# Folding a per-feature norm weight and bias into the product that follows it, and padding the main buffers to multiples of 512 bytes

## The chip, the cores and the metric

The kernel runs on one core of a Trainium2 chip. The metric is device microseconds of one execution; lower is better. Five engines share the work: TensorE (PE), VectorE (DVE), ScalarE (ACT), GpSimd (POOL) and SyncE (SP), which issues most of the DMAs; POOL issues the others. SBUF is the on-chip memory of 128 partitions, and PSUM holds what PE accumulates.

## The reference

One inference step of a two-layer backbone on 128 prompt tokens and 512 latent tokens of width 1024. A layer projects the modulated input, lets four mixers (windowed attention, a gated MLP over chunks, retention, pooling) work on a quarter of the columns each, joins them in an output projection and a layer norm, and ends with a gated convolutional feed-forward network. The change sits in mixer B, the gated MLP:

```
def spatial_gating(u, v, nw, nb, ws, bs):          # u, v: tokens x 256; ws: 4 x 128 x 128; bs: 4 x 128
    v = layer_norm(v, nw, nb)                      # (v - mean) * rstd * nw + nb, over 256 features
    for each chunk of 128 tokens and each head h of 64 features:
        s[i, :] = sum_j ws[h, i, j] * v[j, head h] + bs[h, i]
    return u * s
```

All of it is in fp32.

## The kernel before

The 640 tokens are five tiles of 128 columns (tile 0 is the prompt, tiles 1 to 4 are latent). Activations lie with features on partitions: `y8`, `hh` and `hl` are 128 x 8 x 640. A matmul in fp32 accuracy is made of three with rounded operands: the activation is held as a high part `hh` and a rest `hl`, a weight as `wh` and `wl` (`split`, L275 on ACT and L276 on DVE, from the staging tile `st`), and each product is hh·wh, hh·wl and hl·wh. Lines L601 to L603 (tile `fm`) do so for feature-major outputs, in two pieces of 384 columns (GA) and 256 columns (GB); L883 to L885 (`tm`) for token-major ones; L1497 to L1499 (`wo`) for the output projection; L1588 to L1590 (`dn`) for the feed-forward's second matrix.

The order on each engine is the order in which `mixers` and its helpers are written out; each engine works through its own instructions in that order. Helpers that don't depend on one another run as generators, one piece at every `tick()`.

In mixer B, `sgu_setup` loads the mixing weights, their bias `bs`, and `nwb`: nw and nb copied to all 128 partitions (L742, L743). It transposes the weights on PE (L749) and copies them to SBUF as `wsTs` (ACT, L751). Later `vb_out` takes each token tile's v out of PSUM, `vb_norm` normalizes it in three operations, 128 tokens on partitions by 256 features:

```
V.tensor_scalar(out=v, in0=v, scalar1=mv[:, 0:1], scalar2=r, op0=ALU.subtract, op1=ALU.mult)   # L908, DVE
G.tensor_tensor(out=v, in0=v, in1=m.nwb[:, 0, :], op=ALU.mult)                                 # L909, POOL
G.tensor_tensor(out=v, in0=v, in1=m.nwb[:, 1, :], op=ALU.add)                                  # L910, POOL
```

The factor `r` is one over the standard deviation, a power on POOL (`rstd_of`, L443, tile `rs`). A tile's normalization is written one tile late (`m.owed`), so that on POOL the three kinds stand mixed with the retention gates of `ret_gates` (L1071, L1072), which multiply and add 128 x 128 tiles. `sgu` (L939, tile `sg`) is the mixing on PE, 20 matmuls (40 in the trace's count) for the five tiles; DVE adds `bs` (L942) and `sgu_gate` multiplies with u (L947). The second half of u's product (GB, L601 to L603), one piece of the next layer's modulation matrix (L263, tile `ada`) and the output projection follow on PE.

Of the kernel before, what the change touches and what calls it, by code (L numbers as in the profile page):

```python
# [8 lines left out]
F32 = mybir.dt.float32  # L9
F32R = mybir.dt.float32r  # L10
AF = mybir.ActivationFunctionType
ALU = mybir.AluOpType
AX = mybir.AxisListType

P = 128
# [6 lines left out]
HD = 64  # L22
# [8 lines left out]
NT = 5  # L31
SPLIT_COL = 384
UW = 664

C_ID, C_BD, C_MASK, C_RELF, C_TRIF, C_RELB, C_TRIB = 0, 128, 256, 896, 1024, 1152, 1280
C_IQ, C_KC, C_COS, C_SIN, C_PF = 1408, 1664, 1666, 2178, 2690
# [3 lines left out]
def tcol(t):  # L40
    return t * P
# [48 lines left out]
def kernel(  # L90
# [6 lines left out]
    V, S, G, T = nc.vector, nc.scalar, nc.gpsimd, nc.tensor  # L97
    load, side = nc.sync.dma_start, nc.gpsimd.dma_start

    NW, NU = 12, 25  # L100
    one = ctx.enter_context(tc.tile_pool(name="one", bufs=1))
    par = ctx.enter_context(tc.tile_pool(name="par", bufs=2))
# [9 lines left out]
    def nm(p):  # L112
        cnt[0] += 1
        return f"{p}{cnt[0]}"

    def unit(shape, name="u"):
        u = up.tile([P, UW], F32, tag="u", name=nm(name))[:, 0:math.prod(shape[1:])]
        if len(shape) == 3:
            u = u.rearrange("p (a b) -> p a b", b=shape[2])
        elif len(shape) == 4:  # L120
            u = u.rearrange("p (a b c) -> p a b c", b=shape[2], c=shape[3])
        return u
# [4 lines left out]
    def bank(n=512, name="m"):  # L127
        return pp.tile([P, 512], F32, tag="m", name=nm(name))[:, 0:n]


    ident = one.tile([P, P], F32, name="ident")
    bd = one.tile([P, P], F32, name="bd")
    epsb = one.tile([P, 1], F32, name="epsb")
    mhalf = one.tile([P, 4], F32, name="mhalf")
    hh = one.tile([P, KD, W], F32R, name="hh")
    hl = one.tile([P, KD, W], F32R, name="hl")
    y8 = one.tile([P, KD, W], F32, name="y8")
# [6 lines left out]
    folds = [one.tile([P, 4], F32, name="fold4"), one.tile([P, 2], F32, name="fold2")]  # L144
    sb0 = one.tile([P, 2, KD, 2], F32, name="sb0")
    bf = one.tile([P, 2, KD], F32, name="bf")
    hhf = hh.bitcast(F32)

    V.memset(scT, 0.0)
    V.memset(epsb, EPS)  # L150
    V.memset(mhalf, -0.5)


    class Cols:
        n = 2
# [4 lines left out]
        def dma(self):  # L160
            self.st = stg.tile([P, KD, 256], F32, tag="st", name=nm("st"))
            load(out=self.st, in_=self.src[:, self.c0:self.c0 + 256].rearrange("(k p) c -> p k c", p=P))
# [28 lines left out]
    class AdaFirst:  # L191
# [17 lines left out]
        ps = None  # L209
# [31 lines left out]
    class AdaPair:  # L241

        n = 1
# [155 lines left out]
    def params(l, dma):  # L399
        rows = unit([P, P], name="prow")  # L400
        dma(out=rows[0:16, :], in_=ln_w[l].rearrange("a (m p) -> (a m) p", p=P))
        dma(out=rows[16:32, :], in_=ln_b[l].rearrange("a (m p) -> (a m) p", p=P))
        dma(out=rows[32:34, :], in_=pool_scale[l].rearrange("(m p) -> m p", p=P))
        dma(out=rows[34:38, :], in_=ret_gn_w[l].rearrange("a (m p) -> (a m) p", p=P))
        cr = unit([P, 2, P], name="crow")
        dma(out=cr[0:88, 0, :], in_=ffn_conv_w[l, 0:2].rearrange("t (f p) -> (t f) p", p=P))
        dma(out=cr[0:44, 1, :], in_=ffn_conv_w[l, 2].rearrange("(f p) -> f p", p=P))
        dma(out=cr[44:88, 1, :], in_=ffn_conv_b[l].rearrange("(f p) -> f p", p=P))
        return rows, cr

    def params_tiles():
        return (par.tile([P, 38], F32, tag="prm", name=nm("prm")),
                par.tile([P, 4, 44], F32, tag="cwT", name=nm("cwT")))

    def params2(rc, prm, cwT):
        rows, cr = rc
        pt = bank(name="prT")
        T.transpose(pt[:, 0:38], rows[0:38, :], ident[0:38, 0:38])
        T.transpose(pt[:, 128:216], cr[0:88, 0, :], ident[0:88, 0:88])
        T.transpose(pt[:, 256:344], cr[0:88, 1, :], ident[0:88, 0:88])  # L420
        V.tensor_copy(out=prm, in_=pt[:, 0:38])
        V.tensor_copy(out=cwT[:, 0:2, :], in_=pt[:, 128:216].rearrange("p (t f) -> p t f", t=2))
        V.tensor_copy(out=cwT[:, 2:4, :], in_=pt[:, 256:344].rearrange("p (t f) -> p t f", t=2))

# [181 lines left out]
    def fm_mm(u, lo, hi):  # L606
        return fm_mms([u], lo, hi)[0]
# [124 lines left out]
                         scale=iq[:, 256 + d:257 + d])  # L732
        V.tensor_scalar(out=m.kd, in0=m.kd, scalar1=0.125, scalar2=None, op0=ALU.mult)

    def sgu_setup(m, l):
        w = unit([P, 4, P], name="ws")
        side(out=w, in_=sgu_ws[l].rearrange("h i j -> i h j"))
        m.bs = unit([P, 2, P], name="bs")
        for h in range(4):
            side(out=m.bs[(h % 2) * HD:(h % 2) * HD + HD, h // 2, :], in_=sgu_bs[l, h].partition_broadcast(HD))  # L740
        m.nwb = unit([P, 2, 256], name="nwb")
        side(out=m.nwb[:, 0, :], in_=sgu_nw[l].partition_broadcast(P))  # L742
        side(out=m.nwb[:, 1, :], in_=sgu_nb[l].partition_broadcast(P))  # L743
        yield
        yield
        yield
        pt = bank(name="wsT")
        for h in range(4):
            T.transpose(pt[:, h * P:(h + 1) * P], w[:, h, :], ident)  # L749
        m.wsT = unit([P, 4, P], name="wsTs")  # L750
        S.activation(out=m.wsT, in_=pt.rearrange("p (h i) -> p h i", h=4), func=AF.Copy)  # L751

    def pool_setup(m, l, dma):
        m.pw = par.tile([P, 2, HD], F32, tag="pw", name=nm("pw"))
        dma(out=m.pw, in_=pool_w[l].rearrange("(t a) c d -> (a c) t d", a=2))
        m.pf = par.tile([P, 2, 2, 8], F32, tag="pf", name=nm("pf"))
        dma(out=m.pf, in_=consts[:, C_PF:C_PF + 32].rearrange("p (t e c) -> p t e c", t=2, e=2))
# [144 lines left out]
    def vb_norm(m):  # L902

        if m.owed is None:
            return
        t, v, mv, r = m.owed
        m.owed = None
        V.tensor_scalar(out=v, in0=v, scalar1=mv[:, 0:1], scalar2=r, op0=ALU.subtract, op1=ALU.mult)  # L908
        G.tensor_tensor(out=v, in0=v, in1=m.nwb[:, 0, :], op=ALU.mult)  # L909
        G.tensor_tensor(out=v, in0=v, in1=m.nwb[:, 1, :], op=ALU.add)  # L910
        m.vn[t] = v

    def vc_out(m, t, ps):
# [18 lines left out]
    def sgu(m):  # L932
        for t0, n in ((0, 1), (1, 4)):
            for p in range(2):
                ps = bank(n * P, name="sg")
                for i in range(n):
                    for a in range(2):
                        h = 2 * p + a
                        T.matmul(ps[a * HD:(a + 1) * HD, i * P:(i + 1) * P], m.vn[t0 + i][:, h * HD:(h + 1) * HD],  # L939
                                 m.wsT[:, h, :], start=True, stop=True, tile_position=(0, a * HD))  # L940
                c0 = tcol(t0)
                V.tensor_tensor(out=y8[:, 2 + p, c0:c0 + n * P].rearrange("p (n i) -> p n i", n=n),  # L942
                                in0=ps.rearrange("p (n i) -> p n i", n=n),
                                in1=m.bs[:, p:p + 1, :].to_broadcast([P, n, P]), op=ALU.add)

    def sgu_gate(p, ps, lo, hi):
        V.tensor_tensor(out=y8[:, 2 + p, lo:hi], in0=ps, in1=y8[:, 2 + p, lo:hi], op=ALU.mult)  # L947
# [143 lines left out]
    def pool_in(ps_a, ps_b):  # L1091
        x = unit([P, 664], name="px")
        for a, b in ((0, 8), (136, 144), (656, 664)):
            G.memset(x[:, a:b], 0.0)
        S.activation(out=x[:, 8:136], in_=ps_a[:, 0:P], func=AF.Copy)
        S.activation(out=x[:, 144:400], in_=ps_a[:, P:SPLIT_COL], func=AF.Copy)
        S.activation(out=x[:, 400:656], in_=ps_b, func=AF.Copy)
        return x
# [44 lines left out]
    def lane(*gens):  # L1143
        lanes.append(list(gens))
# [18 lines left out]
    def mixers(l, m, prm, begun=None, aff=None):  # L1163
        dma = side if l else load
# [69 lines left out]
        ps = fm_mm(u, *GA)  # L1234
        S.activation(out=m.kc[0][:, 0:SPLIT_COL], in_=ps, func=AF.Copy)
        tick()
        ps = fm_mm(u, *GB)
# [8 lines left out]
        ps = fm_mm(u, *GA)  # L1246
# [5 lines left out]
        ps = fm_mm(u, *GB)  # L1252
# [6 lines left out]
        for i in range(2):  # L1259
            m.qc.append(keep(unit([P, W], name="qc")))  # L1260
            if i == 0 and aff:
                lane(affine_late(*aff))
        lane(sgu_setup(m, l))
        for d in range(2):
            for p in range(2):
                g = y8[:, 4 + p, :] if d == 0 else unit([P, W], name="g")
                u = ws.take()
                for lo, hi in (GA, GB):
                    ps = fm_mm(u, lo, hi)
                    S.activation(out=g[:, lo:hi], in_=ps, func=AF.Silu)  # L1270
                    if hi == W:
                        G.tensor_scalar(out=g, in0=g, scalar1=prm[:, 34 + d * 2 + p:35 + d * 2 + p], scalar2=None,
                                        op0=ALU.mult)
# [5 lines left out]
        for i in range(2):  # L1279
# [4 lines left out]
            x = pool_in(pa, pb)  # L1284
# [6 lines left out]
        uu = [ws.take(), ws.take()]  # L1291
        pa = [fm_mm(u, *GA) for u in uu]
        sgu(m)
        for p in range(2):
            sgu_gate(p, pa[p], *GA)
# [4 lines left out]
        for p in range(2):  # L1300
            ps = fm_mm(uu[p], *GB)
# [158 lines left out]
    h_first((4, 5, 6, 7), SEG_B, (G, V))  # L1460
    states()
    rc = params(0, load)
    prm, cwT = params_tiles()
    late += [lambda: params2(rc, prm, cwT)]
    load(out=bd, in_=consts[:, C_BD:C_BD + P])

    for l in range(DEPTH):
        m = Mix() if l else m0
# [15 lines left out]
        for h in range(2):  # L1484
# [5 lines left out]
            for t in range(NT):  # L1490
                c0 = tcol(t)
                if h == 0 and 0 < t < NT - 1:
                    y_split(t + 1)
                ps = bank(name="wo")
# [47 lines left out]
        for i, (br, f) in enumerate(order):  # L1542
            u = ws.take()
            ps = fm_mm(u, *GA)
# [22 lines left out]
        if nxt:  # L1567
            rc = params(l + 1, side)
            flush(True)
            sb = mods(adas[l + 1], (prm[:, 8:16], prm[:, 24:32]), 0)  # L1570
# [78 lines left out]
        if nxt:  # L1649
# [3 lines left out]
            prm, cwT = prm2, cwT2  # L1653
# [34 lines left out]
```

## Time and profile before

| what | before |
|---|---|
| median of 3 runs | 1563.03 us (1561.6 to 1563.06) |
| the profiled execution | 1563.34 us, span 1561.6 us |
| PE busy | 1529.7 us, 98% of the span |
| DVE, ACT, POOL busy | 959.5, 609.9, 379.7 us |
| mean granted TensorE clock | 0.994 of full |

The span is the time from the first to the last instruction of the profiled execution. A releaser is what an engine's idle time ended with. The granted clock of a stretch is the share of full speed at which TensorE was let run: 1.00 is 2.4 GHz and 0.50 is 1.2 GHz.

### The profile page before, as it was taken

What the parts mean: (1) busy time and instruction counts of PE and PEld (TensorE: products, weight loads), DVE (VectorE), ACT (ScalarE), POOL (GpSimd) and SP (SyncE); (2) the same over time, 40 slices, a digit from 0 to 9 for tenths busy, and PEclk for the clock granted to TensorE, in tenths of its full rate; (3) what the DMA queues carried; (4) which work ended last, traced back from release to release, by engine and by line L of the source; (5) the groups of instructions that cost most, each with busy time, mean ns of one, the idle gap of its engine ahead of it and who ended that gap; (6) DMA issues with size and microseconds to landing.
All of it is one profiled execution on the core that took longest, in us unless ns stands there. A gap on an engine that the chain in (4) does not pass through costs nothing.

```text
span 1561.6 us, 24577 instructions
## 1 busy us (share of the span) xinstructions
PE 1529.7 (98%) x9734; PEld 1358.4 (87%) x9734; DVE 959.5 (61%) x1891; ACT 609.9 (39%) x993; POOL 379.7 (24%) x458
## 2 busy tenths in 40 slices
PE   8999999999999999999999999899999999999997
PEld 5988878899999999988789988688999999998885
DVE  4775346786556655745577665567866666674456
ACT  2544462344333333533346443524433333343331
POOL 0302266054101101200013033823531101020104
PEclk9999999999999999999999999999999999999999
DMA  9644415245343443333216355161332221224311
GB/s 326 211 152 129 136 55 202 73 130 189 120 151 116 155 137 134 109 117 124 72 38 220 123 163 175 62 202 55 126 104 82 81 81 56 81 93 130 132 38 67
DMA packets 123343, 193.22 MB, mean 124 GB/s; under 512 B 11884, under 2 KB 80566, under 8 KB 123229
## 3 DMA queue, kind: packets, MB, share of 16 engines
q1 hardware_dynamic: 114701, 166.64, 32.1%
q0 software_dynamic: 8528, 25.03, 5.0%
q8 instruction: 76, 1.25, 0.3%
q14 instruction: 38, 0.31, 0.1%
HBM read 177.97 MB, written 13.66 MB: 123 GB/s over the span
## 4 chain that ended last, share of the span: by engine, by line
PE 86%; DVE 4%; POOL 4%; ACT 2%; DMA 2%; issue 1%; SPq 0%; POOLq 0%; ACTq 0%; DVEq 0%
PE fm L601 17%; PE fm L603 16%; PE fm L602 16%; PE dn L1590 6%; PE dn L1588 6%; PE dn L1589 6%; PE ada L263 2%; PE wo L1497 2%; PE wo L1498 2%; PE wo L1499 2%; POOL on L1071 1%; DVE wl L276 1%; PE po L873 1%; PE PT L858 1%; DMA st<-in_w_in_dram 1%
## 5 line engine op out<-in xcount | busy, mean ns | idle before, releaser
L601 PE MATMUL fm<-hh,wh 128*128 128x256 f32 (+1 forms) x1888 | 589.8, 312 | 0.0
L603 PE MATMUL fm<-hl,wh 128*128 128x256 f32 (+1 forms) x1888 | 583.1, 309 | 0.9 <-DVE hl L586 0.9
L602 PE MATMUL fm<-hh,wl 128*128 128x256 f32 (+1 forms) x1888 | 582.9, 309 | 0.0
L276 DVE TENSOR_TENSOR wl<-st,wh 128x1024 fp32r<-128x1024 f32 x188 | 282.7, 1512 | 164.9 <-ACT wh L275 161.8
L601 PEld LDWEIGHTS fm<-hh,wh 128*128 128x128 f32 x1888 | 356.7, 189 | 28.1 <-ACT cv L1328 11.7
L603 PEld LDWEIGHTS fm<-hl,wh 128*128 128x128 f32 x1888 | 356.6, 189 | 1.8 <-DVE hl L586 1.1
L602 PEld LDWEIGHTS fm<-hh,wl 128*128 128x128 f32 x1888 | 356.8, 189 | 0.1
L275 ACT ACTIVATE wh<-st 128x1024 fp32r<-128x1024 f32 x188 | 196.1, 1053 | 207.2 <-PE dn L1589 141.8
L1318 DVE SCALAR_TENSOR_TENSOR cv<-fm,cwT,cv 128x127 f32<-128x127 f32 x352 | 122.0, 408 | 108.3 <-ACT cv L1315 108.2
L1590 PE MATMUL dn<-wh,hl 128*128 128x512 f32 x440 | 174.0, 395 | 0.3 <-DVE hl L1524 0.2
L1588 PE MATMUL dn<-wh,hh 128*128 128x512 f32 x440 | 174.1, 396 | 0.0
L1589 PE MATMUL dn<-wl,hh 128*128 128x512 f32 x440 | 173.8, 395 | 0.0
L1315 ACT ACTIVATE cv<-fm,cwT 128x384 f32<-128x384 f32 x88 | 58.8, 673 | 203.3 <-PE fm L603 187.8
L1537 POOL TENSOR_TENSOR act<-cv,cv 128x640 f32<-128x640 f32 x28 | 45.9, 1641 | 300.3 <-DVE cv L1333 247.3
L1328 ACT ACTIVATE cv<-fm,cwT 128x255 f32<-128x255 f32 x88 | 49.6, 563 | 175.8 <-PE fm L603 175.8
L1590 PEld LDWEIGHTS dn<-wh,hl 128*128 128x128 f32 x440 | 82.5, 187 | 21.4 <-DVE hl L1524 1.2
L1589 PEld LDWEIGHTS dn<-wl,hh 128*128 128x128 f32 x440 | 82.5, 187 | 20.0
L1588 PEld LDWEIGHTS dn<-wh,hh 128*128 128x128 f32 x440 | 82.5, 187 | 19.6
L1329 DVE SCALAR_TENSOR_TENSOR cv<-fm,cwT,bnd 128x1 f32<-128x1 f32 x88 | 19.1, 217 | 89.0 <-ACT cv L1328 88.9
L1537 POOL TENSOR_TENSOR y<-cv,cv 128x640 f32<-128x640 f32 x16 | 26.8, 1678 | 182.3 <-DVE cv L1333 162.6
L1497 PE MATMUL wo<-wh,hh 128*128 128x512 f32 x160 | 64.1, 401 | 0.0
L1498 PE MATMUL wo<-wl,hh 128*128 128x512 f32 x160 | 63.2, 395 | 0.0
(306 smaller groups left out, 2036.1 us busy)
## 6 DMA issues: line engine op xcount, KB each, us to landing
st<-in_ffn_up_dram SPq DMA_DIRECT2D x44, 1024.0 KB
wa<-in_w_ada_dram SPq DMA_DIRECT2D x80, 512.0 KB
st<-in_ffn_down_dram SPq DMA_DIRECT2D x88, 256.0 KB
st<-in_w_in_dram SPq DMA_DIRECT2D x20, 1024.0 KB
xr<-xd POOLq DMA_DIRECT2D x30, 256.0 KB, 8.1
wf<-in_w_first_dram SPq DMA_DIRECT2D x24, 256.0 KB
st<-in_w_out_dram SPq DMA_DIRECT2D x24, 256.0 KB
xd<-xr SPq DMA_DIRECT2D x20, 256.0 KB
```

Of the source, the lines that this page charges most:

```text
L275: S.activation(out=oh, in_=view, func=AF.Copy)
L276: eng.tensor_tensor(out=ol, in0=view, in1=of, op=ALU.subtract)
L601: T.matmul(ps, wh[:, k, :], hh[:, k, lo:hi], start=(k == 0), stop=False)
L602: T.matmul(ps, wl[:, k, :], hh[:, k, lo:hi], start=False, stop=False)
L603: T.matmul(ps, wh[:, k, :], hl[:, k, lo:hi], start=False, stop=(k == KD - 1))
L1318: V.scalar_tensor_tensor(out=o[:, a + d:b - 1 + d], in0=ps[:, a + 1 - d:b - d], scalar=cwT[:, tap, f:f + 1], in1=o[:, a + d:b - 1 + d], op ...
L1497: T.matmul(ps, hh[:, k, c0:c0 + P], wh[:, k % 2, :], start=(k == 0), stop=False)
L1498: T.matmul(ps, hh[:, k, c0:c0 + P], wl[:, k % 2, :], start=False, stop=False)
L1537: G.tensor_tensor(out=dst, in0=a, in1=g, op=ALU.mult)
L1588: T.matmul(ps, hh[:, s_, c0:c0 + P], wh[:, k % 2, :], start=(k == 0), stop=False)
L1589: T.matmul(ps, hh[:, s_, c0:c0 + P], wl[:, k % 2, :], start=False, stop=False)
L1590: T.matmul(ps, hl[:, s_, c0:c0 + P], wh[:, k % 2, :], start=False, stop=(k == KF - 1))
```

## The change

It has two parts. In the first, v is only normalized, and nw and nb come in behind the mixing. Since nw and nb are per feature, the mixing's output is sum_j ws[i, j] * vn[j] times nw, plus nb times the row's sum of ws, plus bs. A feature is a partition there, so nw becomes a per-partition scalar, and the add of L942 becomes one operation that multiplies and adds. The rest, nb times the row sum plus bs, is made once a layer: four matmuls of `wsTs` with a tile of ones (`wsum`) and two operations on DVE. nw and nb come in as four more rows of the small parameter tile `prm`, and `nwb` goes. In the second part two tiles that nothing reads (`pad`, 320 bytes a partition, and `pad2`, 160 bytes) move the addresses of those allocated behind them: in the built program `hh`, `hl` and `y8` began 192 bytes past a multiple of 512 and now begin at one; the staging tiles and the weight tiles wh and wl began 224 bytes past one and now begin at one.

```diff
+PAD1, PAD2 = 80, 40
...
+    pad = one.tile([P, PAD1], F32, name="pad")
     hh = one.tile([P, KD, W], F32R, name="hh")
...
+    pad2 = one.tile([P, PAD2], F32, name="pad2")
+    ones = one.tile([P, HD], F32, name="ones")
+    V.memset(ones, 1.0)
+    for x in (pad, pad2):
+        V.memset(x, 0.0)
...
+        dma(out=rows[38:40, :], in_=sgu_nw[l].rearrange("(m p) -> m p", p=P))
+        dma(out=rows[40:42, :], in_=sgu_nb[l].rearrange("(m p) -> m p", p=P))
...
-    def sgu_setup(m, l):
+    def sgu_setup(m, l, prm):
...
-        m.nwb = unit([P, 2, 256], name="nwb")
-        side(out=m.nwb[:, 0, :], in_=sgu_nw[l].partition_broadcast(P))
-        side(out=m.nwb[:, 1, :], in_=sgu_nb[l].partition_broadcast(P))
...
+        yield
+
+        ps = bank(256, name="wsum")
+        for h in range(4):
+            T.matmul(ps[(h % 2) * HD:(h % 2) * HD + HD, (h // 2) * P:(h // 2) * P + P], ones, m.wsT[:, h, :],
+                     start=True, stop=True, tile_position=(0, (h % 2) * HD))
+        for p in range(2):
+            V.scalar_tensor_tensor(out=m.bs[:, p, :], in0=ps[:, p * P:(p + 1) * P], scalar=prm[:, 40 + p:41 + p],
+                                   in1=m.bs[:, p, :], op0=ALU.mult, op1=ALU.add)
+        m.nw = prm[:, 38:40]
...
-        G.tensor_tensor(out=v, in0=v, in1=m.nwb[:, 0, :], op=ALU.mult)
-        G.tensor_tensor(out=v, in0=v, in1=m.nwb[:, 1, :], op=ALU.add)
...
-                V.tensor_tensor(out=y8[:, 2 + p, c0:c0 + n * P].rearrange("p (n i) -> p n i", n=n),
-                                in0=ps.rearrange("p (n i) -> p n i", n=n),
-                                in1=m.bs[:, p:p + 1, :].to_broadcast([P, n, P]), op=ALU.add)
+                V.scalar_tensor_tensor(out=y8[:, 2 + p, c0:c0 + n * P].rearrange("p (n i) -> p n i", n=n),
+                                       in0=ps.rearrange("p (n i) -> p n i", n=n), scalar=m.nw[:, p:p + 1],
+                                       in1=m.bs[:, p:p + 1, :].to_broadcast([P, n, P]), op0=ALU.mult, op1=ALU.add)
```

On POOL the order in layer 0, at the last two normalizations, was this (`y` is a part of y8 used as scratch, `vn` the normalized v, `g` a retention gate):

```order
L443 TENSOR_TENSOR rs_2546<-rsv_2544,mhalf 128x1
L1071 TENSOR_TENSOR on_2445<-on_2445,y_86 128x128
...
L1072 TENSOR_TENSOR y_86<-on_2445 128x128
L909 TENSOR_TENSOR vn_2484<-vn_2484,nwb_1602 128x256
L910 TENSOR_TENSOR vn_2484<-vn_2484,nwb_1602 128x256
L443 TENSOR_TENSOR rs_2590<-rsv_2588,mhalf 128x1
L909 TENSOR_TENSOR vn_2579<-vn_2579,nwb_1602 128x256
L910 TENSOR_TENSOR vn_2579<-vn_2579,nwb_1602 128x256
L394 DMA gate_2768<-gs_892 128x512
```

In the changed kernel (line numbers are its own) the same place reads:

```order
L452 TENSOR_TENSOR rs_2503<-rsv_2501,mhalf 128x1
L452 TENSOR_TENSOR rs_2552<-rsv_2550,mhalf 128x1
L1085 TENSOR_TENSOR on_2455<-on_2455,y_87 128x128
...
L1086 TENSOR_TENSOR y_87<-on_2455 128x128
L452 TENSOR_TENSOR rs_2594<-rsv_2592,mhalf 128x1
L401 DMA gate_2770<-gs_900 128x512
```

The powers and the gates have kept their order; the ten operations of L909 and L910 in each layer are gone from between them.

On PE the only new rows are those of `wsum`. In layer 1 they stand behind two transposes of attention weights (`PT`), between the two pieces of a projection:

```order
L611 MATMUL fm_9200<-hh,wl_8706 128x384
L612 MATMUL fm_9200<-hl,wh_8705 128x384
L874 MATMUL PT_9226<-ident,P_9039 128x128
L874 MATMUL PT_9226<-ident,P_9045 128x128
L762 MATMUL wsum_9234<-wsTs_9188,ones 64x128 x4
L610 MATMUL fm_9241<-hh,wh_8705 128x256
L611 MATMUL fm_9241<-hh,wl_8706 128x256
```

In layer 0 they stand at the same place of the projection, without the transposes. On DVE the two operations that fold `wsum` into `bs` stand, in layer 0, behind the attention's normalization and ahead of a weight's `wl`:

```order
L865 TENSOR_SCALAR P_1777<-P_1777,su_1849 128x128
L765 SCALAR_TENSOR_TENSOR bs_1605<-wsum_1860,prm_524,bs_1605 128x128 x2
L283 TENSOR_TENSOR wl_1963<-st_1530,wh_1962 128x1024
```

There are 70 microseconds and more between that place and the first use of `bs`.

## Rows read from the trace of the kernel before

**Rows 1.** The page, part 1: TensorE.

```profile
PE 1529.7 (98%) x9734; PEld 1358.4 (87%) x9734; DVE 959.5 (61%) x1891; ACT 609.9 (39%) x993; POOL 379.7 (24%) x458
```

**Rows 2.** Waits of PE: total us, times, longest us.

```profile
PE sg L939 <- POOL vn L910: 7.2, 3, 3.9
...
PE sc L822 <- DVE qs L644: 3.2, 2, 2.4
PE PT L858 <- DVE P L849: 1.6, 1, 1.6
```

**Rows 3.** PE's timeline at both mixings: start, us, instruction, count, idle before.

```profile
241.37 1.31 PE L939 MATMUL sg<-wsTs,vn 128*64 128x128 f32 x20
244.82 1.45 PE L939 MATMUL sg<-wsTs,vn 128*64 128x128 f32 x20 [2.14 <-POOL vn L910]
...
1008.35 1.09 PE L939 MATMUL sg<-wsTs,vn 128*64 128x128 f32 x16
...
1014.99 2.40 PE L939 MATMUL sg<-wsTs,vn 128*64 128x128 f32 x20 [3.89 <-POOL vn L910]
```

**Rows 4.** Stretches: length, busy PE, PEld, DVE, ACT, POOL (counts); clock; DMA share, GB/s.

```profile
82.00:85.41 3.41, 3.41 (x16) 1.63 (x16) 2.28 (x4) 2.85 (x5) 1.46 (x3) 0.50 0.12 42
...
241.37:245.85 4.48, 2.34 (x39) 2.10 (x40) 4.48 (x5) 0.00 (x0) 4.31 (x4) 1.00 0.03 6
245.85:249.26 3.41, 3.41 (x20) 3.10 (x17) 2.52 (x6) 0.78 (x1) 3.25 (x7) 0.50 0.94 257
...
1013.85:1020.68 6.83, 5.69 (x35) 5.36 (x36) 5.20 (x9) 1.51 (x2) 5.88 (x10) 0.50 0.69 166
```

**Rows 5.** PE's timeline behind both mixings: projection GB and the modulation piece.

```profile
249.44 0.28 PE L601 MATMUL fm<-hh,wh 128*128 128x256 f32 x1
...
253.23 0.27 PE L603 MATMUL fm<-hl,wh 128*128 128x256 f32 x1
253.44 1.06 PE L263 MATMUL ada<-wa,scT 128*32 128x512 f32 x8
...
1024.68 1.06 PE L263 MATMUL ada<-wa,scT 128*32 128x512 f32 x8
```

**Rows 6.** POOL's timeline ahead of both mixings.

```profile
239.69 0.74 POOL L910 TENSOR_TENSOR vn<-vn,nwb 128x256 f32<-128x256 f32 x1
240.39 0.55 POOL L443 TENSOR_TENSOR rs<-rsv,mhalf 128x1 f32<-128x1 f32 x1
241.46 1.64 POOL L909 TENSOR_TENSOR vn<-vn,nwb 128x256 f32<-128x256 f32 x1 [0.53 <-DVE vn L908]
243.18 1.58 POOL L910 TENSOR_TENSOR vn<-vn,nwb 128x256 f32<-128x256 f32 x1
...
1010.56 0.55 POOL L443 TENSOR_TENSOR rs<-rsv,mhalf 128x1 f32<-128x1 f32 x1
```

**Rows 7.** DVE's timeline at the last normalization of layer 0, and the projection's activation.

```profile
240.97 0.41 DVE L908 TENSOR_SCALAR vn<-vn,mv,rs 128x256 f32<-128x256 f32 x1 [3.56 <-POOL rs L443]
241.30 4.55 DVE L276 TENSOR_TENSOR wl<-st,wh 128x1024 fp32r<-128x1024 f32 x3
...
249.57 2.36 DVE L1309 TENSOR_TENSOR hl<-y,hh 128x1024 fp32r<-128x1024 f32 x2 [1.21 <-ACT hh L1308]
```

**Rows 8.** Groups of instructions by shape: count | busy us, mean ns | idle before.

```profile
L602 PE MATMUL fm<-hh,wl 128*128 128x384 f32 x928 | 311.9, 336 | 0.0
...
L942 DVE TENSOR_TENSOR y<-sg,bs 128x512 f32<-128x512 f32 x4 | 2.6, 678 | 0.4 <-PE sg L939 0.4
...
L469 DVE SCALAR_TENSOR_TENSOR xr<-xr,rt 128x512 f32<-128x512 f32 x10 | 6.9, 692 | 0.3
...
L823 PE MATMUL sc<-kl,qs 128*128 128x384 f32 x16 | 5.4, 337 | 0.0
```

**Rows 9.** Chain of work that ended last, the opening: start, us, what.

```profile
8.26 11.21 DMA st<-in_w_in_dram
19.50 1.06 ACT wh L275
```

More of the change, by code (lines that the diff above doesn't have):

```diff
@@ L411, in params_tiles @@
     def params_tiles():
-        return (par.tile([P, 38], F32, tag="prm", name=nm("prm")),
+        return (par.tile([P, 42], F32, tag="prm", name=nm("prm")),
                 par.tile([P, 4, 44], F32, tag="cwT", name=nm("cwT")))
@@ L417, in params2 @@
         pt = bank(name="prT")
-        T.transpose(pt[:, 0:38], rows[0:38, :], ident[0:38, 0:38])
+        T.transpose(pt[:, 0:42], rows[0:42, :], ident[0:42, 0:42])
         T.transpose(pt[:, 128:216], cr[0:88, 0, :], ident[0:88, 0:88])
         T.transpose(pt[:, 256:344], cr[0:88, 1, :], ident[0:88, 0:88])
-        V.tensor_copy(out=prm, in_=pt[:, 0:38])
+        V.tensor_copy(out=prm, in_=pt[:, 0:42])
         V.tensor_copy(out=cwT[:, 0:2, :], in_=pt[:, 128:216].rearrange("p (t f) -> p t f", t=2))
@@ L1262, in mixers @@
                 lane(affine_late(*aff))
-        lane(sgu_setup(m, l))
+        lane(sgu_setup(m, l, prm))
         for d in range(2):
```

## The prediction

> **What bounds the kernel.** I read the busy times first. PE works 1529.7 of 1561.6 us [rows 1], so a shorter time needs either a PE idle gap that goes, a stretch at the low clock that goes, or fewer or faster matmuls; POOL and DVE matter only where PE waits for them. Second, what PE waits for: the largest entry is the mixing `sg` behind `vn` of L910 on POOL, 7.2 us in three waits [rows 2]. That is the place that the change touches, once in each layer. Third, PE's timeline there. In layer 0 the mixing starts at 241.37, stops for 2.14 us and is over at about 246.2; in layer 1 it starts at 1008.35 and its longest stop is 3.89 us [rows 3].
>
> Fourth, the granted clock by stretch. Behind the stop of layer 0 the clock is 0.50 from 245.85 to 249.26, and in layer 1 it is 0.50 from 1013.85 to 1020.68, the end of the stop included [rows 4]. Level 0.50 is 1.2 GHz, 1.00 is 2.4 GHz. The stretch from 82.00 to 85.41, also 3.41 us, likewise lies behind a PE wait, that of `sc` for DVE [rows 2, 4]. So each stop costs twice: once as idle time, once as slow matmuls.
>
> **What the two places cost now.** From the first `sg` to the piece `ada` that follows projection GB, layer 0 takes 253.44 − 241.37 = 12.07 us, layer 1 1024.68 − 1008.35 = 16.33 us [rows 3, 5]. Without stops and at the full clock, the same work is: 40 `sg` records at 1.31 us for 20, or 2.62 us [rows 3]; and 48 matmuls of GB. Thirty-three of these run at the full clock from 249.44 to 253.23, 32 steps in 3.79 us or 0.118 us each [rows 5], so 48 take 5.69 us. Together 8.31 us. The excess is 3.76 us in layer 0 and 8.02 us in layer 1, 11.8 us in all. The other way to reckon it agrees: 7.2 us of waits, plus half of the low-clock time in which PE worked (3.41 us, and 5.69 busy of 6.83 us, [rows 4]), 4.6 us, is also 11.8 us.
>
> **Does the stop go?** What `sg` waits for is the last tile's chain: power on POOL (240.39), normalization on DVE (240.97), L909 and L910 on POOL (241.46 and 243.18, 1.64 and 1.58 us) [rows 6, 7]. The last two operations go, 3.2 us directly in each layer. The power itself also comes earlier: four pairs of L909 and L910 stood ahead of it in POOL's order, at 0.74 us an operation [rows 6] 8 × 0.74 = 5.9 us. POOL was busy nearly without a break there, so I let the power move by about 5 us, since with POOL freer the powers begin to wait for DVE's statistics instead. In layer 0 it then ends near 236 and the normalization near 236.5, 5 us before PE comes to `sg`. In layer 1 the power at 1010.56 [rows 6] moves to about 1005.5 and the normalization to 1006.5, some 2 us ahead of 1008.35. So I expect no stop in either layer, with the smaller margin in layer 1. Had the removed pair alone gone and nothing moved up, `vn` would be ready near 241.4 and 1011.6, and layer 1 would still stop: there it is the moving up that decides.
>
> What is late next? On DVE the three `wl` of 4.55 us [rows 7] stand behind the last normalization; they move up with it and end near 241 and 1011, about where `sg` ends (241.37 + 2.62 = 244.0; 1008.35 + 2.62 = 1011.0). Then come the four operations of L942 (two short ones and two of 0.68 us, [rows 8], about 1.9 us), the two gates of 384 columns (about 0.5 us each at L942's rate), and `hh` on ACT and `hl` on DVE for one token tile, 128 x 1024 (1.06 us for a `wh` of that size in [rows 9], 1.2 us as half of the 2.36 us in [rows 7]): 5.1 us behind `sg` or, in layer 1, behind 1011. PE meanwhile has GB and `ada`, 5.69 + 1.06 us, before the output projection asks for `hl`. That leaves 1.6 us to spare. The staging tiles that these `wl` release come free earlier too, so the loads of the output projection's weights start earlier, not later.
>
> **What is added.** PE: `wsum` is four matmuls of a 128 x 64 stationary tile against 128 columns, the same form as `sg`, where 20 records take 1.31 us; eight records are 0.52 us a layer, 1.0 us in all, if nothing hides them. In layer 0 a PE wait of 1.6 us for the attention's normalization, `PT` behind `P` [rows 2], lies shortly after them and can take them in, so the bounds are 0.5 and 1.0 us; I take 0.8. Their input `wsTs` is made by ACT about a projection's GA (some 4 us) earlier, so I price that wait at nothing; without the cover it would be under 1 us. DVE: two operations of 128 x 128 a layer, no dearer than the short ones of L942, on an engine that is idle 39% of the time [rows 1]. L942 turns from an add into a multiply-and-add: on 128 x 512 the nearest rows are 678 ns for L942 itself and 692 ns for L469, which multiplies and adds [rows 8], so 0.01 us each. Two small DMAs more go into SP's queue in layer 0 ahead of the convolution's parameters, and two of `nwb` leave POOL's queue. The parameters are transposed on PE once per layer, where a late landing would cost at most the issue of the two, about 0.6 us; I take nothing, and keep 0.6 for the range.
>
> **The padding.** It moves where every operand of about 1530 us of PE work begins. Per matmul, the trace has a comparison: in `sc` (L823) the moving operand `kl` begins, by the built program's addresses, at 0, 320 or 384 past a multiple of 512; its 384-column matmuls take 337 ns on average, and those of `fm`, which begin at 192, take 336 ns [rows 8]. So I price the padding at nothing on PE. The stationary operand and the engines' writes have no such row. Bounds: if it gave or cost 1 ns for each of the about 7500 large matmuls (5664 of `fm`, 1320 of `dn`, 480 of `wo`), that would be 7.5 us either way; the two means above differ by 1 ns.
>
> A row that DMA could move is in the opening: the first staging tile's load takes 11.21 us and ACT starts right behind it [rows 9]. The Trainium skill, "DMA: Bandwidth & Descriptors", section "How a descriptor splits into AXI transactions", says that a descriptor which does not start on a 256-byte boundary fetches the bytes before it too, and that these cost beats. By that rule a piece of 1024 bytes beginning at 224 would need 39 beats of 32 bytes where an aligned one needs 32 (an estimate from that page), and the opening would be some 2 us shorter. No row here compares loads into the two kinds of places at the same load on the engines. By rows alone it is a bound: each tenth off the 11.21 us is 1.1 us. I leave it out of the sum.
>
> **The sum.** −11.8 + 0.8 = −11.0 us. Against the profiled execution's own 1563.34 us that is 1552.3; its time is 0.3 us over the median of the runs, so for the median about 1552.
>
> **Rivals.**
> Some of the cost stays (16 in 100). Either the layer-1 normalization is still late because the powers now wait for DVE, or the clock still falls though the stop is gone. For it: a margin of only 2 us there, and `sg` is light work for PE. Against: from 241.37 to 245.85 the clock stayed at 1.00 through `sg` and the stop [rows 4], and fell only behind it. If the waits alone go, −7.2 + 0.8 gives 1556.6; if layer 0 alone is cured, −3.8 + 0.8 gives 1560.
>
> The padding makes matmuls quicker (7 in 100). The equal means of `sc` and `fm` speak against it. From 1 ns a matmul on it would show, 1552 − 7.5 = 1544.5, and lower from there.
>
> The opening's load gets quicker (8 in 100), because the staging tile begins at a multiple of 512: a tenth to a fifth off 11.21 us is 1.1 to 2.2 us, so 1550 to 1551.
>
> The gain is given back behind the mixing (7 in 100): the chain of L942, gates, `hh`, `hl` is longer than I have it, PE stops ahead of the output projection, and the clock falls there instead. Each microsecond late costs one, and a low stretch like that of 82 us another 1.7, so giving back 8 to 11 us ends within 0.2% of before.
>
> Slower than before (8 in 100): the aligned places cost PE. All operands of a matmul now begin at the same place within 512 bytes, which they did not do before (192 for activations, 224 for weights). `sc` says nothing on the weights. It decides from (11.0 + 3.1)/7500 = 1.9 ns a matmul on: 1566 and more. Against it stand the equal means.
>
> **Chances and range.** My forecast, stops and low clock gone and padding without effect, has 54 in 100 and lies between 1550 and 1555. A measurement can tell about 0.2% (3.1 us) from no change. Faster by more than that (under 1559.9) holds the forecast, most of the first rival, the two quick ones: 54 + 13 + 7 + 8 = 82, less 1 for what I have not seen; within it 10; slower 9. For 8 in 10 the range runs from 1546 to 1561, which leaves out the quicker matmuls and the slower case and the worst of what is given back.
>
> **What would show it.** Right: no entry `sg` behind `vn` of POOL or DVE in PE's waits; 8.3 to 8.9 us from the first `sg` to `ada` in both layers; a clock of 1.00 in the stretches behind; POOL about 16 us less busy (20 operations at 0.74 to 1.64 us, 18 us, and nothing added); `fm` means unchanged at 336 ns for 384 columns. Wrong: a stop ahead of `wo`, a new low-clock stretch elsewhere, or means of `fm`, `dn` and `wo` that moved by more than 1 ns.

## The result and the profile after

The changed kernel takes 1544.49 us (median of 4 runs, 1542.55 to 1545.73) against 1562.78 us before (4 runs): ratio 0.9884, 95% interval 0.987 to 0.9899, or 18.3 us less. I had forecast 1552 and a range from 1546 to 1561. The profiled execution took 1544.51 us, 18.8 us less than that of before.

First part 1 of the page of the changed kernel:

```profile
PE 1520.0 (99%) x9750; PEld 1361.0 (88%) x9750; DVE 958.7 (62%) x1898; ACT 609.3 (40%) x993; POOL 361.6 (23%) x436
```

POOL lost 18 us of work and PE 10 us of busy time against [rows 1]. Then what PE waits for (us, times, longest):

```profile
PE ada L223 <- ACT scT L1434: 6.0, 1, 6.0
PE sc L838 <- DVE qs L653: 3.0, 2, 2.3
...
PE PT L874 <- DVE P L865: 0.8, 1, 0.8
```

The entry of `sg`, 7.2 us before [rows 2], is gone, and none has come in its place. Next, PE's timeline at the mixing and the modulation piece of each layer:

```profile
240.88 2.40 PE L953 MATMUL sg<-wsTs,vn 128*64 128x128 f32 x40
249.16 1.06 PE L270 MATMUL ada<-wa,scT 128*32 128x512 f32 x8
...
1001.47 2.40 PE L953 MATMUL sg<-wsTs,vn 128*64 128x128 f32 x40
...
1009.74 1.07 PE L270 MATMUL ada<-wa,scT 128*32 128x512 f32 x8
```

The stretches of projection GB between them (columns as in [rows 4]):

```profile
243.50:249.16 5.66, 5.66 (x49) 5.53 (x48) 4.45 (x7) 2.96 (x3) 1.96 (x4) 1.00 1.03 321
1004.10:1009.74 5.64, 5.64 (x48) 5.51 (x46) 4.43 (x7) 2.96 (x3) 2.47 (x5) 1.00 1.02 292
```

From `sg` to `ada` it is 8.28 us in layer 0 and 8.27 us in layer 1, where it was 12.07 and 16.33 [rows 3, 5]; the clock behind is 1.00 where it was 0.50 [rows 4]. The two places give 11.85 us. The end of the chain ahead of the mixing in layer 1, the last normalization on DVE:

```profile
997.91 0.41 DVE L924 TENSOR_SCALAR vn<-vn,mv,rs 128x256 f32<-128x256 f32 x1 [2.04 <-POOL rs L452]
```

It ends at 998.32, 3.1 us ahead of the mixing. That leaves some 7 us of the 18.8 for which the fold has no row. They are in the large matmuls. From here on a step is the time from the start of one matmul to the start of the next; they overlap, so it is shorter than the time shown for one. The first and last row of an unbroken run of `dn` on PE, in the same phase of layer 0, before and after:

```profile
660.52 0.39 PE L1588 MATMUL dn<-wh,hh 128*128 128x512 f32 x1
...
699.95 0.39 PE L1589 MATMUL dn<-wl,hh 128*128 128x512 f32 x1
```

```profile
659.65 0.39 PE L1604 MATMUL dn<-wh,hl 128*128 128x512 f32 x1
...
700.00 0.39 PE L1602 MATMUL dn<-wh,hh 128*128 128x512 f32 x1
```

Before, 169 steps take 39.43 us, 233.3 ns each; after, 178 steps take 40.35 us, 226.7 ns each. This is a difference of 6.6 ns for every 512-column matmul, and there are 1320 of `dn` and 480 of `wo`: 11.9 us, if each gained as much. Not all forms gained. The groups by shape of the changed kernel (count | busy us, mean ns):

```profile
L611 PE MATMUL fm<-hh,wl 128*128 128x384 f32 x928 | 310.4, 334 | 0.0
L611 PE MATMUL fm<-hh,wl 128*128 128x256 f32 x960 | 271.1, 282 | 0.0
L1603 PE MATMUL dn<-wl,hh 128*128 128x512 f32 x440 | 171.3, 389 | 0.0
L900 PE MATMUL tm<-wl,hh 128*128 128x256 f32 x160 | 45.7, 286 | 0.0
```

In the kernel before, the same groups have means of 336, 282, 395 and 280 ns: `dn` lost 6 ns, `tm` gained 6. Projection GB of layer 0 shows the 256-column `fm` in detail: 118.3 ns a step before (32 steps [rows 5]), 119.8 after (46 steps from 243.44 to 248.95). Over all unbroken rows of the trace at the full clock the mean step of 256-column `fm` rose from 118.2 to 119.6 ns and that of `tm` from 117.1 to 119.6, while that of 384-column `fm` stayed at 173.6 to 173.7. With 2880, 480 and 2784 matmuls this gives back 4.0 and 1.2 us of the 11.9 and leaves 6.7, about what the fold left open. So the new addresses moved the step of each form by its own amount and with its own sign.

### The profile page after: what moved, and what is told of

Its sections match the earlier page's. It is cut to its first block, busy times and chain, and to the rows that moved or that the text cites. A ratio compares the mean times of both kernels' runs of the same rounds, so it can differ in the third digit from the quotient of the medians.

```text
span 1542.4 us, 24589 instructions
## 1 busy us (share of the span) xinstructions
PE 1520.0 (99%) x9750; PEld 1361.0 (88%) x9750; DVE 958.7 (62%) x1898; ACT 609.3 (40%) x993; POOL 361.6 (23%) x436
## 4 chain that ended last, share of the span: by engine, by line
PE 90%; DVE 5%; ACT 2%; issue 1%; DMA 1%; POOL 0%; SPq 0%; POOLq 0%; ACTq 0%; DVEq 0%
PE fm L610 17%; PE fm L612 16%; PE fm L611 16%; PE dn L1604 6%; PE dn L1602 6%; PE dn L1603 6%; PE ada L270 3%; PE wo L1511 2%; PE wo L1513 2%; PE wo L1512 2%; PE tm L899 1%; PE tm L900 1%; PE tm L901 1%; DVE wl L283 1%; PE po L889 1%
## 5 line engine op out<-in xcount | busy, mean ns | idle before, releaser
L1513 PE MATMUL wo<-wh,hl 128*128 128x512 f32 x160 | 62.4, 390 | 0.0
```

Of the source, the lines that this page charges most:

```text
L1513: T.matmul(ps, hl[:, k, c0:c0 + P], wh[:, k % 2, :], start=False, stop=(k == KD - 1))
```

## The experiments

Unless said otherwise each computes what the reference does. "Places" are bytes past a multiple of 512 at which `hh`, `hl`, `y8` (the activations) and the staging and weight tiles begin: 192 and 224 before, 0 and 0 in the changed kernel. A ratio is against the kernel before, run beside it, with its 95% interval in brackets. Edits are shown in part, with "..." for the rest; what stands behind a # is a note.

### The two parts apart

`fold_only` is the changed kernel with the old places; `pads_only` is the kernel before with the new ones.

```diff
 fold_only, against the changed kernel
-PAD1, PAD2 = 80, 40
+PAD1, PAD2 = 0, 48       # places 192 and 224
...
-    pad = one.tile([P, PAD1], F32, name="pad")
 pads_only, against the kernel before
+    pad = one.tile([P, 80], F32, name="pad")       # ahead of hh
...
+    pad2 = one.tile([P, 120], F32, name="pad2")    # behind the last single tile: places 0 and 0
```

> The fold of nw and nb alone, with hh, hl and y8 left at 192 and the staging and weight tiles at 224 past a multiple of 512, as before. If the fold gives what its terms say (11.8 us of waits and low clock less 1.2 us for wsum), 1552 us, ratio 0.993, and dn and wo matmuls start every 234 ns as before. If the extra 7 to 8 us came from the fold too (a later stage that now runs closer), about 1545 us, ratio 0.988.

> The kernel before with the two pads alone: hh, hl, y8, staging and weights begin at multiples of 512, the norm stays where it was. If the padding makes the 512-column matmuls quicker (234 to 227 ns in dn and wo, some 1800 of them, less about 2 us that tm loses), about 1555 us, ratio 0.995, with both stops of sg still there. If the padding does nothing by itself, 1562.8 us, ratio 1.000.

Measured: `fold_only` 1552.04 us (the kernel before, beside it, 1562.03), ratio 0.9937 (0.9924 to 0.9949); `pads_only` 1553.83 us, ratio 0.9949 (0.9936 to 0.9963). In the first, PE has no wait at `sg` and `dn` steps as before, 172 steps in 40.14 us, 233.4 ns:

```profile
659.80 0.40 PE L1602 MATMUL dn<-wl,hh 128*128 128x512 f32 x1
...
699.94 0.40 PE L1603 MATMUL dn<-wh,hl 128*128 128x512 f32 x1
```

In the second, `dn` steps every 226.7 ns (177 steps), and the waits of `sg` are all there:

```profile
659.79 0.39 PE L1592 MATMUL dn<-wh,hh 128*128 128x512 f32 x1
...
699.91 0.39 PE L1592 MATMUL dn<-wh,hh 128*128 128x512 f32 x1
```

```profile
PE sg L943 <- POOL vn L914: 6.8, 3, 3.9
```

The fold is worth 10.0 us and the padding 8.2; the sum, 18.2, is the whole. As far as intervals of some 2 us either way can tell, they are two independent changes.

### Which tile's place decides

Here the changed kernel has one of the two groups put back.

```diff
-PAD1, PAD2 = 80, 40
+PAD1, PAD2 = 0, 120      # fold_hh192_w0 (the tile pad goes): activations 192, weights 0
...
+PAD1, PAD2 = 80, 96      # fold_hh0_w224: activations 0, weights 224
```

> The changed kernel with hh, hl and y8 back at 192 past a multiple of 512; staging and weights stay at multiples of 512. If the start of the moving weights decides, dn and wo stay at 227 ns and tm at 120 ns, about 1544 us, ratio 0.988. If the start of the stationary activations decides, dn and wo return to 234 ns and the time to about 1552 us, ratio 0.993.

> The changed kernel with staging and weights back at 224 past a multiple of 512; hh, hl and y8 stay at multiples of 512. If the start of the moving weights decides, dn and wo return to 234 ns and tm to 117 ns, about 1552 us, ratio 0.993. If the start of the stationary activations decides, dn and wo stay at 227 ns, about 1544 us, ratio 0.988. If both have to be aligned, this one and the run with hh at 192 both come out near 1552 us.

Measured: activations at 192 and weights at 0, 1531.59 us, ratio 0.9804 (0.9791 to 0.9818), 13 us under the changed kernel; activations at 0 and weights at 224, 1552.46 us, ratio 0.9935 (0.9922 to 0.9948). The first agrees with neither theory: it is better than both aligned. The `dn` runs of the two, 228.9 ns (175 steps) and 233.3 ns (172 steps):

```profile
659.78 0.39 PE L1602 MATMUL dn<-wl,hh 128*128 128x512 f32 x1
...
699.84 0.39 PE L1603 MATMUL dn<-wh,hl 128*128 128x512 f32 x1
```

```profile
659.81 0.40 PE L1604 MATMUL dn<-wh,hl 128*128 128x512 f32 x1
...
699.94 0.40 PE L1602 MATMUL dn<-wh,hh 128*128 128x512 f32 x1
```

So with activations at 192, `dn` gives a third of its gain back, and the 13 us come from elsewhere, the 256-column `fm`. Its group in the run with activations at 192:

```profile
L610 PE MATMUL fm<-hh,wl 128*128 128x256 f32 x960 | 266.0, 277 | 0.0
```

Its mean is 277 ns, from 282; in projection GB it steps every 113.3 ns (46 steps from 243.09 to 248.30), 6.5 ns under the changed kernel. Over all 2880 of them the mean step is 114.2 ns, from 119.6, which is 15.6 us; 1800 of 512 columns at 2.2 ns lose 4.0, and `tm` (117.5 ns, from 119.6) gains 1.0: 12.6 us of the 13. Two theories had fallen: that one operand's own place decides, and that multiples of 512 are best. What was left is the place of one operand against the other.

### A map of both places

`map` does nothing of the reference's work. It runs rows of 16 equal matmuls, with the moving operand (the one that streams through PE) at one of 16 places (ma to mp) and the stationary one (the one that PE holds) at one of 16 (sa to sp), 32 bytes apart; for 384 columns it takes every second letter of both. From 21 us to the end of the last row the other engines are idle.

```diff
+    ms = [one.tile([P, 1032], F32R, name="m" + x) for x in letters]    # 4128 bytes each: 32 more every time
...
+    ss = [one.tile([P, 520], F32R, name="s" + x) for x in letters]     # 2080 bytes each
...
+    for m in ms:
+        for s in ss:
+            run512(m, s)       # 16 matmuls, s in slices of 512 bytes, m of 2048
```

> Not the reference's work: nothing but rows of 16 equal matmuls on two arenas, 512, 384 and 256 columns, for 16 places of the moving operand (ma to mp, 0 to 480 past a multiple of 512 in steps of 32) by 16 places of the stationary one (sa to sp, the same). If the moving operand's start decides, a row's time depends on the letter of m alone, 512 columns near 227 ns a matmul for ma and near 233 ns for mh (224). If the start of both against each other decides, it changes with the letter of s too, and the quick pairs lie along a line of equal distance between m and s. If the start has nothing to do with it, and only what the other engines read at the time, all pairs take the same.

PE's timeline of some rows of 512 columns and, behind them, of 256. In a row's name the moving operand stands first; a row's step is the difference of its start and the next row's, over 16:

```profile
94.02 3.84 PE L122 MATMUL big<-mb,sh 128*128 128x512 f32 x16
97.70 3.89 PE L122 MATMUL big<-mb,si 128*128 128x512 f32 x16
101.42 3.80 PE L122 MATMUL big<-mb,sj 128*128 128x512 f32 x16
105.06 3.89 PE L122 MATMUL big<-mb,sk 128*128 128x512 f32 x16
...
134.78 3.80 PE L122 MATMUL big<-mc,sc 128*128 128x512 f32 x16
...
227.58 3.80 PE L122 MATMUL big<-md,sl 128*128 128x512 f32 x16
...
1561.69 2.00 PE L134 MATMUL low<-mo,sa 128*128 128x256 f32 x16
1563.53 2.08 PE L134 MATMUL low<-mo,sb 128*128 128x256 f32 x16
...
1576.81 2.05 PE L134 MATMUL low<-mo,si 128*128 128x256 f32 x16
1578.69 2.04 PE L134 MATMUL low<-mo,sj 128*128 128x256 f32 x16
```

The quick rows (3.80 us) are mb with sj, md with sl, eight letters or 256 bytes on, and mc with sc, 0 bytes on. Rows six letters on, 192 bytes (mb with sh, 3.84 us), come second. Averaged over the steps inside a row, 512 columns take 226.7 ns where the stationary operand begins 0 bytes past the moving one (counted within 256), 229.5 ns at 192, and 232.3 to 233.7 ns at the other six distances, whatever the places themselves; rows right behind a change of the moving tile differ from these by up to 2 ns, and the very first row, whose steps are longer than 400 ns up to 10.4 us, is left out. The theory of the distance holds and the other two fall. For 256 columns the means go from 117.1 ns (224) to 119.4 (160), but there the distance is not all: at 64, mo with sa steps by 1.84 us over 16, 115 ns, and mo with si by 1.88 us, 117.5 ns. Of the 32 rows at 64 six are as quick as the first, and all six stand within the first five rows behind a change of the moving tile, so what ran just before may count too; no run tells.

Now the kernels can be read. In `dn` the weight moves and the activation is stationary: the distance is 192 − 224, or 224 within 256, before; 0 after; 192 with activations at 192 and weights at 0; 32 with weights at 224. The map's 233.2, 226.7, 229.5 and 233.0 ns stand against the measured 233.3, 226.7, 228.9 and 233.3. For 256 columns `fm` (activation moving, weight stationary) and `tm` (the other way round) have mean steps in these kernels of 119.6 ns at 0, 118.2 at 32, 117.5 at 192 and 117.0 to 117.1 at 224, where the map has 119.3, 118.2, 117.8 and 117.1. At 64 it fails: 256-column `fm` takes 114.2 ns where most rows of the map take 117.9, and 384-column `fm` 173.7 where the map has 176.7.

### The distance, at other places

`both_at_96` keeps the distance 0 at a place that is a multiple of 32 only; `hh0_w64` keeps the distance of the quick run at other places.

```diff
-PAD1, PAD2 = 80, 40
+PAD1, PAD2 = 104, 40     # both_at_96
+PAD1, PAD2 = 80, 56      # hh0_w64: activations 0, weights 64
```

> The changed kernel with hh, hl, y8, staging and weights all 96 bytes past a multiple of 512: the distance between activations and weights is 0 as in the changed kernel, but nothing begins at a multiple of 512 or of 64. If the distance decides, 1544.5 us, ratio 0.988, with dn and wo at 227 ns and 256-column fm at 119.5 ns. If beginning at multiples decides, 1552 us, ratio 0.9935, with dn at 233 ns.

> The changed kernel with hh, hl and y8 at a multiple of 512 and staging and weights 64 bytes past one: the same distance of weights from activations, 64 within 256, as in the run with hh at 192 and weights at 0. If the distance decides, 1531.6 us as there, ratio 0.980, with 256-column fm at 114.2 ns and dn between 228 and 231 ns. If beginning at multiples of 512 decides, at least as slow as with weights at 224, 1552 us; if multiples of 64 do, as the changed kernel, 1544.5 us.

Measured: `both_at_96` 1546.03 us, ratio 0.9901 (0.9887 to 0.9914), `dn` at 226.7 ns (177 steps in 40.12 us); `hh0_w64` 1532.6 us, ratio 0.9824 (0.9801 to 0.9847; one of its five runs took 1540.75), projection GB at 113.3 ns a step. Both are where the distance puts them, and neither agrees with multiples of 512 or 64. The rows are those of `both_at_96`.

```profile
659.81 0.39 PE L1604 MATMUL dn<-wh,hl 128*128 128x512 f32 x1
...
699.93 0.39 PE L1604 MATMUL dn<-wh,hl 128*128 128x512 f32 x1
```

### A distance for each use

`best` makes the weight tiles 256 bytes longer and lets a unit's data begin where its use is quickest. The two pads go, and the tile of ones with its 256 bytes moves into a rotating unit.

```diff
+    def wtile(shape, dt, off, name):
+        t = wp.tile([P, D + 64], dt, tag="w", name=nm(name))[:, off:off + D]
+        return t if len(shape) == 1 else t.rearrange("p (a b) -> p a b", b=shape[1])
...
-        wh = wp.tile([P] + list(shape), F32R, tag="w", name=nm("wh"))
+        off = {KD: 56, 4: 48, 2: 40}[shape[0]]        # fm, tm, dn and wo
+        wh = wtile(shape, F32R, off, "wh")
...
```

> The fold without pads, with weight tiles 256 bytes longer, in which a unit's data begins where the map has each use quickest: weights 64 past the activations (within 256) for the feature-major products, 0 for dn and wo, and activations 224 past the weights for tm; the tile of ones lies in a rotating unit. If the distance decides for each product by itself, 256-column fm 114.2 ns, dn and wo 226.7 ns, tm 117.1 ns: about 4 us under the run with hh at 192 and weights at 0, 1527 us, ratio 0.978. If the longer tiles cost elsewhere, or a product's time hangs on more than its own pair, 1532 us or more.

Measured: 1530.18 us, ratio 0.9805 (0.9784 to 0.9826). The steps are those expected, `dn` 226.7 ns over 177 steps and GB 113.5 ns, and the groups have the means of the quickest kernels above:

```profile
L610 PE MATMUL fm<-hh,wl 128*128 128x256 f32 x960 | 266.0, 277 | 0.0
L1604 PE MATMUL dn<-wl,hh 128*128 128x512 f32 x440 | 171.4, 389 | 0.0
```

Its runs (1527.22 to 1536.91) scatter more than those of the run with activations at 192 and weights at 0, and the two intervals overlap. That it is the quicker of the two is not shown; that both beat the changed kernel is.

### Only the last pair off the path

`fold_last_pair` is `fold_only` with two multiplications by one on POOL for tiles 0 to 3, so that the power of the last tile comes as late as the pairs ahead of it make it.

```diff
         V.tensor_scalar(out=v, in0=v, scalar1=mv[:, 0:1], scalar2=r, op0=ALU.subtract, op1=ALU.mult)
+        if t < NT - 1:
+            for _ in range(2):
+                G.tensor_tensor(out=v, in0=v, in1=ones[:, 0:1].to_broadcast([P, 256]), op=ALU.mult)
```

> The fold alone (places as before), with two multiplications by one left on POOL for tiles 0 to 3 where the two operations of the norm stood, so that only the last pair is taken out of the way. If moving the power up is what decides in layer 1, the mixing of layer 0 has no stop and that of layer 1 still has one, of 2 to 3 us behind the normalization, perhaps with a low clock behind it: 1554 to 1557 us, ratio 0.995 to 0.997. If taking out the last pair is enough, 1552 us as with the fold alone, ratio 0.994.

Measured: 1557.7 us, ratio 0.9976 (0.9965 to 0.9987), 5.7 us over `fold_only`. But the mixing has no stop; the wait stands some 25 us further on, at the output projection, as PE's waits show:

```profile
PE wo L1515 <- DVE hl L1325: 3.5, 2, 2.8
```

The timeline of layer 1: the mixing, the three `wl` behind the last normalization on DVE, SP's loads of the output projection's weights, ACT, and PE's wait:

```profile
1004.85 2.71 PE L955 MATMUL sg<-wsTs,vn 128*64 128x128 f32 x40
...
1006.11 3.49 DVE L282 TENSOR_TENSOR wl<-st,wh 128x1024 fp32r<-128x1024 f32 x3
...
1008.49 11.10 SPq L188 DMA_DIRECT2D st<-in_w_out_dram  x10
...
1020.56 1.06 ACT L281 ACTIVATE wh<-st 128x1024 fp32r<-128x1024 f32 x1 [5.12 <-DMA st<-in_w_out_dram]
1024.27 1.06 ACT L281 ACTIVATE wh<-st 128x1024 fp32r<-128x1024 f32 x1 [2.65 <-DMA st<-in_w_out_dram]
1025.23 2.93 ACT L1324 ACTIVATE hh<-y 128x1024 fp32r<-128x1024 f32 x3
...
1029.82 0.50 PE L1515 MATMUL wo<-wh,hl 128*128 128x512 f32 x1 [2.76 <-DVE hl L1325]
```

The same rows of `fold_only`:

```profile
1002.85 3.49 DVE L282 TENSOR_TENSOR wl<-st,wh 128x1024 fp32r<-128x1024 f32 x3
...
1005.23 11.76 SPq L188 DMA_DIRECT2D st<-in_w_out_dram  x10
...
1021.97 2.94 ACT L1321 ACTIVATE hh<-y 128x1024 fp32r<-128x1024 f32 x3
```

The `wl` start 3.3 us later, although PE comes to the mixing 1.2 us earlier here (1006.04 in `fold_only`); the loads into the staging tiles that they release are issued 3.3 us later, ACT waits in order for what they bring, and the `hh` of the next token tiles, queued behind, is 3.3 us later too. `hl` follows `hh`, and PE waits for it: 2.76 us here, and 0.78 at the output projection of layer 0. For `hh` itself it waits 0.46 us. The clock of the 5 us from 1029 on is 0.68, with 3.41 us at 0.50, which cost half of that. Together this is 5.7 us. Both theories of this run fall in part: the later power does cost, but through this chain, which I had not followed. Nor is it the whole delay of the old order: in layer 1 the two multiplications take 1.3 us where L909 and L910 took 1.5, and the last normalization ends at 1006.19, 1.3 us behind the start of the mixing, where the prediction has it 3.2 us behind if only the last pair goes. Whether the mixing would stop then is not shown.

## Why the prediction was wrong, by its steps

**The stop and the clock: right.** The excess of 11.8 us was 11.85, the 8.31 us of clean work 8.28 and 8.27. The last normalization of layer 1 ended 3.1 us ahead of the mixing, where I had some 2.

**What is added: right within half a us.** `wsum` takes 0.6 us a layer, from its start to the next `fm`, so 1.2 us, and the wait of `PT` fell from 1.6 to 0.8 us, which takes in layer 0's part. I had 0.8 in all. With the fold alone the kernel took 10.0 us less, and my sum without the padding was 11.0; that its 1552.04 us is my 1552 to the digit is luck, as the kernel before was 1.0 us quicker beside it. In the profiled execution of `fold_only` the stretch at the low clock behind the wait of `sc`, 2.4 us as before, was longer by 3.4 us than before (last section), which costs 1.7 us.

```profile
165.51 0.66 PE L762 MATMUL wsum<-wsTs,ones 128*64 128x128 f32 x8
166.10 0.39 PE L610 MATMUL fm<-hh,wh 128*128 128x256 f32 x1
```

**The padding: this step failed.** I put it into the sum as nothing and priced it "at nothing on PE" because `sc`, with moving operands at 0, 320 and 384, and `fm`, at 192, have the same mean [rows 8]. Those rows compare the moving operand's own place, in 384 columns; the map's settled steps there run only from 173.3 to 176.7 ns. What decides is the distance to the stationary operand, and where it shows most is in 512 and 256 columns, which I did not compare. The padding alone was worth 8.2 us: 6.6 ns on each of 1800 matmuls of 512 columns, less what `fm` and `tm` of 256 columns gave back. The bound that I gave, 1 ns a matmul or 7.5 us either way, came near in total, but the forms moved by -6.6, +1.4, +2.5 and +0.1 ns, each its own way; the error was to carry one form's equal means over to all forms, and so to take the bound as nearly symmetric noise around nothing and give the quicker side 7 in 100.

**The rivals.** The one that came true is the quicker matmuls. That its 1544.5 us is the time measured is luck: it is 1 ns on each of 7500 matmuls, where the runs showed 6.6 on 1800 and a loss on others. It named no reason; the one that the change suggests, alignment, is not it. The slower rival, both operands "at the same place within 512 bytes", named the condition that matters for `dn` and `wo`, with the wrong sign: at distance 0 they are quickest. It holds for `tm` and 256-column `fm`, which became slower. The opening's load is 10.51 us where it was 11.21 [rows 9], and 10.51 to 10.83 in three kernels with staging at 0, against 10.87 to 11.39 in six with it elsewhere (before, `fold_only`, `fold_last_pair`, weights at 224, both at 96, `best`), one execution each. That agrees in sign with the Trainium skill's rule ("DMA: Bandwidth & Descriptors", "How a descriptor splits into AXI transactions") but is some 0.6 us on average, not the 2 that I had estimated from it. The page speaks of bytes that are fetched, and here it is the place written to that moved; the two groups lie only 0.04 us apart, so that the place causes it is not shown. What was to be given back behind the mixing was not: PE has no wait at `wo`. `fold_last_pair` shows how near that rival lay.

## What to carry to other kernels

When a change moves addresses, compare matmuls of every shape by their start-to-start step over a long unbroken run, not one shape by its mean; a few ns on thousands of matmuls is more than a stop of an engine. On this chip look at the distance between the starts of the moving and the stationary operand, not at their alignment. A small map gave the right distance for 512 columns; for 256 and 384 it missed what the kernel did at 64, so the last word is the step measured in the kernel. And when an operation moves up, follow what its release lets other queues start: the wait of a late power did not show where the power was used, but 25 us on.

## What was not expected of the hardware

- The step of an fp32r matmul (of rounded operands such as `wh` and `hh`) depends on the distance, within 256 bytes, between the places where its two operands begin: 226.7 to 233.7 ns for 512 columns. Why is not shown; that PE loads the next stationary operand while it streams the moving one is a guess at where the two could meet.
- At 256 columns the same distance, 64, gave two steps in the map, 115 and 117.5 ns for the two rows shown, and 113.3 ns in projection GB. What else decides there stays open.
- A wait of PE is not always followed by a low clock. In `pads_only` `sg` waited 1.91 us in layer 0, ahead of its second half at 243.28, and the clock of the stretch around it stayed at 1.00 (columns as in [rows 4]); in the kernel before, 2.14 us at the same place were followed by 3.41 us at 0.50. Behind the wait of `sc` for `qs`, 2.3 to 2.4 us each time, the clock was at 0.50 for 3.41 us in the kernel before and the changed one, for 6.83 us in `fold_only`, and not at all in `both_at_96` and `best`. Such a stretch costs about half its length (in that of `fold_last_pair` `wo` steps by 0.43 us, against 0.23 outside), so one profiled execution can differ from another by 1.7 to 3.4 us for this alone, as much as the intervals leave open above. The rows are the stop in `pads_only` and its stretch, then `fold_only` and `both_at_96` behind `sc`.

```profile
243.28 1.31 PE L943 MATMUL sg<-wsTs,vn 128*64 128x128 f32 x20 [1.91 <-POOL vn L914]
...
239.00:252.00 13.00, 11.09 (x105) 9.40 (x104) 11.37 (x15) 2.96 (x3) 9.04 (x13) 1.00 0.58 161
...
81.15:87.98 6.83, 6.56 (x29) 4.78 (x30) 5.13 (x11) 4.14 (x8) 1.67 (x3) 0.50 0.16 61
...
81.88:88.71 6.83, 6.83 (x56) 5.92 (x57) 5.42 (x13) 4.14 (x9) 1.67 (x3) 1.00 0.12 44
```
